# Three pairs of k-tiles by seven products in most FFN groups, with the sums of weights on GpSimd

## The chip, the core and the metric

The kernel runs on one core of one Trainium2 chip. The metric is device time in microseconds; three runs of the kernel before took 1980.76, 1980.84 and 1981.82 us, median 1980.84. The core's engines are named in the profile PE (TensorE, matmuls) with PEld (its weight loads), DVE (VectorE), ACT (ScalarE), POOL (GpSimd) and SP (SyncE, which here only issues loads and stores).

## The reference: one decoder block

On 256 positions of width 2048, all in fp32, one layer is computed:

```python
h = h + 0.5 * swiglu(rms_norm(h, ffn1_norm), ffn1_w_gu, ffn1_w_down)
h = h + hybrid_mixer(rms_norm(h, mix_norm), w_in, ..., w_out)
h = h + 0.5 * swiglu(rms_norm(h, ffn2_norm), ffn2_w_gu, ffn2_w_down)
h = h + sigmoid(rms_norm(h, ple_norm) @ ple_w_gate) * (p @ ple_w_proj)
out = rms_norm(h, final_norm)
```

`swiglu(x)` splits `x @ w_gu` into a gate and an up half of 5632 columns each and gives `(silu(gate) * up) @ w_down`. The two FFNs are most of the work, and the change concerns them alone.

## The kernel before

**Precision.** Every fp32 operand of a large matmul is split in two pieces of the type fp32r, a rounded copy "hi" and the difference "lo". A product of two operands is three matmuls: hi by hi, hi by lo, lo by hi. For weights this is `weight_pair` (L57): a load of 128x2x512 weights (a pair of k-tiles, 512 columns, 512 KB) into `raw`, a copy `whi` on ScalarE (L68) and a difference `wlo` on VectorE (L69). There are four buffers for `raw` and three each for `whi` and `wlo`.

**Groups.** An FFN is a list of groups (`plan`, L325). A gate/up group computes 512 columns of the gate and the 512 matching ones of up, for all 256 positions: 2 column blocks x 2 halves of the positions, four PSUM banks, with 8 pairs of k-tiles per block. The 11 such groups stand in three parts (`PARTS`, L27) of 3, 4 and 4; after each part two down groups multiply that part's hidden columns (12 or 16 pairs of k-tiles over two blocks) into 1024 columns of the output each. A plain pair is 2 k-tiles x 2 halves of the positions x 3 = 12 matmuls (L445 to L447).

**Seven products.** For the first `NS` = 2 pairs of k-tiles of a group the eight block products (2 halves of the positions x 2 k-tiles x 2 column blocks) are replaced by seven products of sums, in Strassen's manner: four sums of the activations, four of the weights, and additions of results into the PSUM banks. Each of the seven is 3 matmuls per pair of k-tiles (L311 to L313). The first two gate/up groups of FFN 1 and the first of FFN 2 have no such products.

- `halves` (L369) makes the activations' sums `S` on VectorE (L375, L382) and their pieces `Sh` and `Sl` (L385, L386), once for the FFN's input and once for the first hidden block of each part.
- `Group.load` (L263) loads the raw weights of the pairs into `R0` and `R1` with four 512 KB loads (L268). `all_sums` (L270) is a generator: each step yields the pieces `shi` (ScalarE, L277) and `slo` (VectorE, L278, two buffers each) of one product's weights; between the steps stand four additions on VectorE (L282), one of them into `R0`, one into `R1`, two into a tile `t2`.
- `product` (L300) issues the matmuls of one product and, after products 2, 3 and 4, the additions of one bank to another: a copy `part` on ScalarE (L318), an addition on VectorE (L319).

**The order.** A group's seven products are issued among the plain pairs of the group ahead of it, from that group's fourth pair on, one behind each pair. The list `order` names all weights of the kernel in the order of their use: pairs, sums and loads of raw weights. `next_weights` (L76) hands out the next one and prepares up to three pairs and two sums ahead. `lanes` holds generators for the work beside the matmuls; each is advanced by one step per pair. The framework puts the instructions of one engine in the order in which they are ready by its own plan, so `shi` of a coming group's first product stands on ScalarE ahead of `whi` of pairs that come earlier in `order`. Each engine then runs its instructions in that order. All loads of weights are issued from SP's queue.

Of the kernel before, what the change touches and what calls it, by code (L numbers as in the profile page):

```python
# [28 lines left out]
NS = 2  # L29
# [8 lines left out]
def block_kernel(ctx, tc, a, out):  # L38
# [37 lines left out]
    def next_weights():  # L76

        ahead = min(LEAD, done[1] // 2)
        while done[0] < len(order):
# [4 lines left out]
            if kind == "load":  # L84
                src.load()
# [153 lines left out]
    class Group:  # L239
# [8 lines left out]
        def __init__(self, kind, part, src, ns, bank, nb=0):  # L248
            self.kind, self.part, self.src, self.ns, self.nb, self.bank = kind, part, src, ns, nb, bank
            self.last = part == len(PARTS) - 1  # L250
# [12 lines left out]
        def load(self):  # L263
            fp = current[0]
            self.raw = [fp.tile([P, NS, 2, NB], F32, tag=f"R{b}", name=f"R{b}") for b in range(2)]
            for g in range(NS):
                for b in range(2):
                    nc.sync.dma_start(out=self.raw[b][:, g], in_=self.src[b][g])  # L268

        def all_sums(self):  # L270

            fp = current[0]

            def halved(w):
                hi = fp.tile([P, NS, NB], F32R, tag="shi", name="shi", bufs=2)
                lo = fp.tile([P, NS, NB], F32R, tag="slo", name="slo", bufs=2)
                nc.scalar.copy(hi, w)  # L277
                nc.vector.tensor_tensor(out=lo, in0=w, in1=hi, op=ALU.subtract)  # L278
                return hi, lo

            def add(out, x, y):
                nc.vector.tensor_tensor(out=out, in0=x, in1=y, op=ALU.add)  # L282
# [12 lines left out]
            ws = halved(b21)  # L295
            add(t2, t2, b21)
            yield ws
            yield halved(b22)
            yield halved(t2)

        def product(self, i):
# [4 lines left out]
            out = (c11, c21, c12, c22, c11, c12, c21)[i]  # L306
            whi, wlo = next_weights()
            for g in range(NS):
                xh, xl = sides[self.kind](i, g)
                st, sp = i < 4 and g == 0, i < 4 and g == NS - 1  # L310
# [18 lines left out]
    def plan(n):  # L329

        gu, down = a["w_gu" + n], a["w_down" + n]
        groups = []
        for p, (i0, i1) in enumerate(PARTS):
            for i in range(i0, i1):
                groups.append(Group("gu", p, [[gu[2 * i + b][g] for g in range(KD // 2)] for b in range(2)],
                                    NS if i > (n == "1") else 0, len(groups) % 2))
            for nb in (0, 2):
                groups.append(Group("dn", p, [[down[nb + b][g] for g in range(2 * i0, 2 * i1)] for b in range(2)],
                                    NS, len(groups) % 2, nb))
        made = []  # L340
        for i, group in enumerate(groups):
            group.follower = follower = groups[i + 1] if i + 1 < len(groups) else None
            first = 3 if i else 8
            at = []
            if follower is not None and follower.ns:
                free = len(group.plain) - 2 - first
                at = [first + min(j, j * free // 7) for j in range(7)]
            todo = []
            for j, (b, g) in enumerate(group.plain):
                if at and j == max(at[0] - 5, 0):  # L350
                    order.append(("load", follower))
                todo.append(("plain", (b, g)))
                order.append(("pair", group.src[b][g]))
                for x in range(7):
                    if at and at[x] == j:
                        todo.append(("seventh", x))
                        order.append(("sum", follower))
            made.append((group, todo))
# [10 lines left out]
    def halves(kind, hi, lo, wait=0):  # L369

        for _ in range(wait):
            yield
        fp = current[0]
        x = fp.tile([P, 2, 4, P], F32, tag="tT", name="tT").rearrange("p t q y -> p (t q y)")
        nc.vector.tensor_tensor(out=x, in0=hi.bitcast(F32).rearrange("p k x -> p (k x)"),  # L375
                                in1=lo.bitcast(F32).rearrange("p k x -> p (k x)"), op=ALU.add)
        x = x.rearrange("p (g j t y) -> p g j t y", g=NS, j=2, t=2)
        a11, a12, a21, a22 = (x[:, :, j, t, :] for t in range(2) for j in range(2))
        s = fp.tile([P, 4, NS, P], F32, tag="S", name="S")
        for o, y, z, op in ((0, a21, a22, ALU.subtract), (1, s[:, 0], a11, ALU.subtract),  # L380
                            (2, a21, a11, ALU.subtract), (3, s[:, 1], a12, ALU.add)):
            nc.vector.tensor_tensor(out=s[:, o], in0=y, in1=z, op=op)  # L382
        sh = fp.tile([P, 4, NS, P], F32R, tag="Sh" + kind, name="Sh")
        sl = fp.tile([P, 4, NS, P], F32R, tag="Sl" + kind, name="Sl")
        nc.scalar.copy(sh, s)  # L385
        nc.vector.tensor_tensor(out=sl, in0=s, in1=sh, op=ALU.subtract)  # L386

        def side(i, g):
            if i in (0, 4, 6):
                k, t = 2 * g + (i > 0), i // 6  # L390
# [822 lines left out]
```

## Time and profile before

The profiled execution took 1982.68 us, of which the profile's span is 1981.0. How many instructions of each kind there are and what they cost is asked of the trace by line, engine and shape; "mean" is the time from the start to the end of one instruction, and consecutive ones overlap somewhat. The four additions of L282 have a row each.

| what | count | mean ns | busy us |
|---|---|---|---|
| `whi`, ACT L68, 128x1024 | 583 | 1053 | 613.3 |
| `wlo`, DVE L69, 128x1024 | 583 | 1221 | 710.5 |
| `shi` of raw weights or sums in `R`, ACT L277 | 155 | 1054 | 163.3 |
| `slo` of the same, DVE L278 | 155 | 1222 | 189.3 |
| additions to `R` and `t2`, DVE L282 | 4 x 31 | 1203 to 1225 | 37.3 to 38.0 each |
| additions between banks, DVE L319 | 124 | 693 to 694 | 84.9 |

In the page's rows of 40 slices each digit is a tenth of the slice's time in which the engine was busy; PEclk is the granted clock of TensorE, which is full in every slice. POOL's row holds one 1 and 39 zeros, so GpSimd is all but idle. In rows of waits the first name is the waiting instruction's, the second the one that released it, then come the total, the number of times and the longest, in us.

### The profile page before, as it was taken

The numbers are of one execution on the slowest core, as the hardware profiler recorded it, in microseconds if no ns is written. First come the engines' busy times: TensorE is split into PE (matmuls) and PEld (weight loads), VectorE is DVE, ScalarE is ACT, GpSimd is POOL, SyncE is SP. The second block draws the span as 40 slices with busy tenths as digits, with TensorE's granted clock in tenths as the row PEclk, the third lists the DMA queues.
The fourth block names the chain that finished last, engine by engine and source line by source line (L and its number), as shares of the span: only waits on it lengthen the run. The fifth ranks groups of instructions, "written<-read, shape, count | busy, mean of one in ns | idle before, by whom it ended". The sixth has DMA issues, their size and how long they took to land. (4 is left out here: it accounts for less than half of the span.)

```text
span 1981.0 us, 24832 instructions
## 1 busy us (share of the span) xinstructions
PE 1961.9 (99%) x9022; PEld 1621.5 (82%) x9022; DVE 1507.4 (76%) x1803; ACT 1116.1 (56%) x1441; POOL 30.1 (2%) x46
## 2 busy tenths in 40 slices
PE   9999999999999999999999999999999999999998
PEld 7888888888888888878878888888888888888887
DVE  6878788777887766794786677888787877887655
ACT  6655555555555557654545455665565555655654
POOL 0000000000000000000100000000000000000000
PEclk9999999999999999999999999999999999999999
DMA  9666667756667665555564786665667656665764
GB/s 329 225 222 212 217 209 227 237 186 212 230 215 226 203 210 163 175 179 193 171 206 148 248 269 209 228 230 195 215 217 245 213 192 210 225 225 198 241 206 151
DMA packets 163228, 421.64 MB, mean 213 GB/s; under 512 B 20512, under 2 KB 59424, under 8 KB 162976
## 3 DMA queue, kind: packets, MB, share of 16 engines
q1 hardware_dynamic: 161952, 418.58, 64.2%
q10 hardware_dynamic: 1152, 1.47, 0.2%
q8 instruction: 71, 1.16, 0.2%
q14 instruction: 53, 0.43, 0.1%
HBM read 397.96 MB, written 22.02 MB: 212 GB/s over the span
## 5 line engine op out<-in xcount | busy, mean ns | idle before, releaser
L68 ACT CAST whi<-raw 128x1024 fp32r<-128x1024 f32 (+1 forms) x585 | 614.5, 1052 | 716.8 <-PE u L447 168.4
L69 DVE TENSOR_TENSOR wlo<-raw,whi 128x1024 fp32r<-128x1024 f32 (+1 forms) x585 | 711.9, 1220 | 372.0 <-ACT whi L68 370.9
L446 PE MATMUL g<-wlo,nTh 128*128 128x512 f32 x552 | 216.0, 391 | 0.4 <-DVE wlo L69 0.4
L445 PE MATMUL g<-whi,nTh 128*128 128x512 f32 x552 | 215.2, 391 | 0.7 <-ACT whi L68 0.7
L447 PE MATMUL g<-whi,nTl 128*128 128x512 f32 x552 | 215.8, 391 | 0.0
L445 PE MATMUL u<-whi,nTh 128*128 128x512 f32 x552 | 214.7, 389 | 0.0
L446 PE MATMUL u<-wlo,nTh 128*128 128x512 f32 x552 | 214.7, 389 | 0.0
L447 PE MATMUL u<-whi,nTl 128*128 128x512 f32 x552 | 214.7, 389 | 0.0
L445 PE MATMUL d<-whi,hTh 128*128 128x512 f32 x512 | 199.1, 389 | 1.0 <-ACT hTh L414 1.0
L446 PE MATMUL d<-wlo,hTh 128*128 128x512 f32 x512 | 199.2, 389 | 0.0
L447 PE MATMUL d<-whi,hTl 128*128 128x512 f32 x512 | 199.2, 389 | 0.0
L278 DVE TENSOR_TENSOR slo<-R,shi 128x1024 fp32r<-128x1024 f32 x155 | 189.3, 1222 | 12.6 <-ACT shi L277 2.7
L277 ACT CAST shi<-R 128x1024 fp32r<-128x1024 f32 x155 | 163.3, 1054 | 34.7 <-PE d L313 14.2
L103 PE MATMUL pj<-whi,nTh 128*128 128x512 f32 x448 | 179.5, 401 | 0.0
L104 PE MATMUL pj<-wlo,nTh 128*128 128x512 f32 x448 | 176.0, 393 | 2.3 <-DVE wlo L69 2.1
L105 PE MATMUL pj<-whi,nTl 128*128 128x512 f32 x448 | 175.3, 391 | 0.0
L446 PEld LDWEIGHTS g<-wlo,nTh 128*128 128x128 f32 x552 | 104.0, 188 | 23.7 <-DVE wlo L69 2.1
L445 PEld LDWEIGHTS g<-whi,nTh 128*128 128x128 f32 x552 | 104.0, 189 | 22.6 <-ACT whi L68 1.0
L447 PEld LDWEIGHTS g<-whi,nTl 128*128 128x128 f32 x552 | 104.0, 188 | 21.9 <-DVE nTl L153 0.4
L447 PEld LDWEIGHTS u<-whi,nTl 128*128 128x128 f32 x552 | 103.6, 188 | 21.6
L446 PEld LDWEIGHTS u<-wlo,nTh 128*128 128x128 f32 x552 | 103.6, 188 | 21.5
L445 PEld LDWEIGHTS u<-whi,nTh 128*128 128x128 f32 x552 | 103.6, 188 | 21.5
(301 smaller groups left out, 3028.3 us busy)
## 6 DMA issues: line engine op xcount, KB each, us to landing
raw<-in_w_gu SPq DMA_DIRECT2D x275, 512.0 KB, 4.2
raw<-in_w_down SPq DMA_DIRECT2D x128, 512.0 KB, 3.7
raw<-in_w_in SPq DMA_DIRECT2D x112, 512.0 KB, 3.6
R<-in_w_gu SPq DMA_DIRECT2D x76, 512.0 KB, 5.4
R<-in_w_down SPq DMA_DIRECT2D x48, 512.0 KB, 5.6
scr<-tb SPq DMA_DIRECT2D x74, 256.0 KB, 4.0
raw<-in_w_out SPq DMA_DIRECT2D x32, 512.0 KB, 4.2
raw<-in_w_pg SPq DMA_DIRECT2D x32, 512.0 KB, 4.4
```

Of the source, the lines that this page charges most:

```text
L68: nc.scalar.copy(hi[:, j, :], raw[:, j, :])
L69: nc.vector.tensor_tensor(out=lo[:, j, :], in0=raw[:, j, :], in1=hi[:, j, :], op=ALU.subtract)
L103: nc.tensor.matmul(outs[t], xh[:, c], whi[:, j, :], start=st, stop=False)
L104: nc.tensor.matmul(outs[t], xh[:, c], wlo[:, j, :], start=False, stop=False)
L105: nc.tensor.matmul(outs[t], xl[:, c], whi[:, j, :], start=False, stop=sp)
L277: nc.scalar.copy(hi, w)
L278: nc.vector.tensor_tensor(out=lo, in0=w, in1=hi, op=ALU.subtract)
L445: nc.tensor.matmul(out, xh[:, c], whi[:, j, :], start=st, stop=False, skip_group_check=True)
L446: nc.tensor.matmul(out, xh[:, c], wlo[:, j, :], start=False, stop=False, skip_group_check=True)
L447: nc.tensor.matmul(out, xl[:, c], whi[:, j, :], start=False, stop=sp, skip_group_check=True)
```

## The change

- `NS` becomes 3: three pairs of k-tiles go by seven products in all gate/up groups that have products, and in the down groups of the two parts of four; the down groups of the first part stay at two (`NS_DOWN`). A product is then 9 matmuls, and a group of 16 pairs has 10 plain pairs.
- The weights of those pairs are laid out in memory so that each of the four quarters (k-tile j of the pair, column block b) of all pairs is one load of 128x1536 (768 KB), tiles `R00` to `R11`. The quarters of a group are loaded while the group two places ahead of it computes, behind products 5 and 6.
- The seven products come in another order, and the weights' sums are made in place in the quarters, without `t2`; the four additions are issued on GpSimd. Both additions that used to follow products 2 and 3 in the banks now follow product 2, and the two of product 4 follow product 3.
- Products start behind the third pair of the group ahead.
- `halves` goes through its operands two pairs at a time, and its results for the FFN's input and for the hidden columns share one buffer, so they are made anew when the kind changes: at the last gate/up group and at the second down group of a part.

```diff
-NS = 2
+NS = 3
+NS_DOWN = tuple(3 if i1 - i0 == 4 else 2 for i0, i1 in PARTS)
...
+        def load(self, j, b):
+            self.raw[j, b] = raw = current[0].tile([P, NS, NB], F32, tag=f"R{j}{b}", name="R")[:, 0:self.ns]
+            nc.sync.dma_start(out=raw, in_=self.quarters[b][j])
+        def loads(self):
+            return [("load", lambda j=j, b=b: self.load(j, b)) for j, b in ((0, 1), (1, 0), (0, 0), (1, 1))]
...
-            def add(out, x, y):
-                nc.vector.tensor_tensor(out=out, in0=x, in1=y, op=ALU.add)
-            (b11, b21), (b12, b22) = ([r[:, :, j, :] for j in range(2)] for r in self.raw)
-            ws = halved(b11)
-            add(b11, b11, b12)
-            t2 = fp.tile([P, NS, NB], F32, tag="t2", name="t2")
-            add(t2, b11, b22)
-            yield ws
-            yield halved(t2)
-            ws = halved(b11)
-            add(b12, b12, b22)
-            yield ws
-            yield halved(b12)
-            ws = halved(b21)
-            add(t2, t2, b21)
-            yield ws
-            yield halved(b22)
-            yield halved(t2)
+            def add(x, y):
+                nc.gpsimd.tensor_tensor(out=self.raw[x], in0=self.raw[x], in1=self.raw[y], op=ALU.add)
+            for q, sum_ in (((0, 0), ((0, 0), (0, 1))), ((0, 0), ((0, 0), (1, 1))), ((0, 0), ((0, 1), (1, 1))),
+                            ((0, 1), ((0, 0), (1, 0))), ((1, 0), None), ((0, 0), None), ((1, 1), None)):
+                ws = halved(*q)
+                if sum_:
+                    add(*sum_)
+                yield ws
...
-            out = (c11, c21, c12, c22, c11, c12, c21)[i]
+            out = (c11, c12, c21, c22, c11, c21, c12)[i]
...
             if i == 2:
                 add(c21, c11, ALU.add)
+                add(c12, c21, ALU.subtract)
             elif i == 3:
-                add(c12, c21, ALU.subtract)
-            elif i == 4:
                 add(c21, c22, ALU.subtract)
                 add(c22, c12, ALU.add)
...
-            first = 3 if i else 8
+            after = groups[i + 2] if i + 2 < len(groups) else None
...
+                first = 2 if group.ns else 8
+                at = [first + j * (n_plain - 1 - first) // 7 for j in range(7)]
+                if not group.ns:
+                    loads.setdefault(max(at[0] - 5, 0), []).extend(follower.loads())
+                if after is not None and after.ns:
+                    for x, one in zip((5, 6, 7, 7), after.loads()):
+                        loads.setdefault(at[x] if x < 7 else min(at[6] + 1, n_plain - 1), []).append(one)
...
-        sh = fp.tile([P, 4, NS, P], F32R, tag="Sh" + kind, name="Sh")
-        sl = fp.tile([P, 4, NS, P], F32R, tag="Sl" + kind, name="Sl")
+    def halves(kind, his, los, ns, wait=0):
+        sh = fp.tile([P, 4, NS, P], F32R, tag="Sh", name="Sh")
+        sl = fp.tile([P, 4, NS, P], F32R, tag="Sl", name="Sl")
+        for g0 in range(0, ns, 2):
...
+                if dn and group.nb and not group.last:
+                    lanes.add(1, halves("gu", *nT, NS))
+                elif not dn and group.follower.kind == "dn":
+                    lanes.add(1, halves("dn", hTh[i0:], hTl[i0:], NS_DOWN[group.part]))
```

More of the change, by code (lines that the diff above doesn't have):

```diff
@@ L329, in plan, with sources @@
     def plan(n):
[L331 removed]
+        def sources(name, blk):
+            q, pairs = a[name + "q"][blk], a[name][blk]
+            return [q[:, :, g, :].rearrange("j p n -> p j n") for g in range(q.shape[2])] + \
+                [pairs[g] for g in range(pairs.shape[0])], q
         groups = []
@@ L357, in plan @@
                         order.append(("sum", follower))
+                order.extend(loads.get(j, []))
             made.append((group, todo))
@@ L479, in ffn @@
                             lanes.advance(0)
-                        if len(hTh) - 1 == PARTS[group.part][0]:
-                            lanes.add(0, halves("dn", th, tl))
         return nxt
```

89 lines of the change are left out of this document (45 added, 44 removed).

## The prediction

> **What bounds the kernel now.** I read the page's busy shares first, then a table of three stretches that are each one FFN group long, then the groups of instructions, the waits and the short timelines below.
>
> ```profile
> span 1981.0 us, 24832 instructions
> ## 1 busy us (share of the span) xinstructions
> PE 1961.9 (99%) x9022; PEld 1621.5 (82%) x9022; DVE 1507.4 (76%) x1803; ACT 1116.1 (56%) x1441; POOL 30.1 (2%) x46
> ```
>
> The profiled execution took 1982.68 us, of which 1981.0 are the span; the median of the timed runs is 1980.84, so span and median can be read as one. TensorE is busy in 99% of it and waits for nobody worth naming: what takes matmuls away shortens the kernel, as long as the other engines keep up. Whether they do is seen in the stretches:
>
> ```profile
> core 0: us, PE busy (x) PEld busy (x) DVE busy (x) ACT busy (x) POOL busy (x), PEclk, DMA share, GB/s
> 191.17:222.66 31.49, 31.49 (x140) 25.75 (x138) 27.16 (x27) 17.61 (x19) 0.00 (x0) 1.00 0.62 211
> 475.62:517.78 42.16, 42.16 (x188) 34.91 (x186) 32.33 (x31) 23.08 (x25) 0.00 (x0) 1.00 0.64 205
> 1237.52:1279.68 42.16, 42.16 (x188) 34.91 (x186) 36.63 (x39) 24.89 (x28) 0.00 (x0) 1.00 0.67 224
> ```
>
> Each row runs from one group's product 0 to the next group's: a down group of the first part (12 pairs in all), a gate/up group (16 pairs) and one in which the operand sums of `halves` are made as well. TensorE is full in all three. A group of 16 pairs holds 12 plain pairs of 12 matmuls and 7 products of 6, so 186 in 42.16 us: 0.2267 us each, a plain pair 2.72. VectorE has 9.8 us to spare out of 42.2 in the second row, 4.3 out of 31.5 in the first. GpSimd does nothing there.
>
> ```profile
> DVE wlo L69 <- ACT whi L68: 370.9, 316, 3.6
> ACT whi L68 <- PE u L447: 168.4, 135, 2.0
> ```
>
> The spare time of VectorE is waiting of this kind: it waits for ScalarE's `whi`, and that for the plain pair whose buffer (one of three) it takes. So VectorE is as far ahead as buffers allow, some two pairs, and is idle because it is ahead.
>
> ```profile
> 328.94 1.06 ACT L277 CAST shi<-R 128x1024 fp32r<-128x1024 f32 x1 [0.30 <-PE u L313]
> 331.66 1.06 ACT L68 CAST whi<-raw 128x1024 fp32r<-128x1024 f32 x1 [1.66 <-PE u L447]
> ```
>
> The same holds for a sum's pieces: `shi` starts when the product that had its buffer, two products earlier, ends (L313 is a product's last matmul). Of a product with number i, copy, difference and addition therefore have to fit between the end of product i-2 and the start of product i.
>
> **TensorE's part.** The number of groups that get a third pair follows from the loads of raw weights, four a group:
>
> ```profile
> R<-in_w_gu SPq DMA_DIRECT2D x76, 512.0 KB, 5.4
> R<-in_w_down SPq DMA_DIRECT2D x48, 512.0 KB, 5.6
> ```
>
> 76/4 = 19 gate/up groups and 48/4 = 12 down groups, of which the 8 in the two parts with four column blocks get three pairs and the 4 of the first part stay at two. In each of the 27, two plain pairs go (24 matmuls) and seven products grow from 6 matmuls to 9 (21): 3 fewer, 81 in all, 81 x 0.2267 = 18.4 us. The group's TensorE time becomes 10 x 2.72 + 7 x 2.04 = 41.5 us.
>
> **VectorE's part.** What a group of it costs:
>
> ```profile
> L69 DVE TENSOR_TENSOR wlo<-raw,whi 128x1024 fp32r<-128x1024 f32 x583 | 710.5, 1221 | 371.0 <-ACT whi L68 370.1
> L278 DVE TENSOR_TENSOR slo<-R,shi 128x1024 fp32r<-128x1024 f32 x155 | 189.3, 1222 | 12.6 <-ACT shi L277 2.7
> ...
> L282 DVE TENSOR_TENSOR t<-R,R 128x1024 f32<-128x1024 f32 x31 | 38.0, 1225 | 1.0
> L282 DVE TENSOR_TENSOR R<-R,R 128x1024 f32<-128x1024 f32 x31 | 38.0, 1224 | 3.7 <-DMA R<-in_w_gu 2.8
> L282 DVE TENSOR_TENSOR R<-R 128x1024 f32<-128x1024 f32 x31 | 37.8, 1219 | 0.0
> L282 DVE TENSOR_TENSOR t<-t,R 128x1024 f32<-128x1024 f32 x31 | 37.3, 1203 | 0.0
> L319 DVE TENSOR_TENSOR d<-d,part 128x512 f32<-128x512 f32 x48 | 32.1, 693 | 0.0
> ```
>
> Removed: the four additions, 4 x 1.22 = 4.9 us, and two `wlo`, 2.4. Added: `slo` on 1536 elements instead of 1024; from 693 ns at 512 and 1222 at 1024 the slope is 1.03 ns per element, so +0.53 each, 7 x 0.53 = 3.7. The second row's 32.3 becomes 32.3 - 4.9 - 2.4 + 3.7 = 28.7 us of 41.5. Taken alone, VectorE gets lighter. ScalarE, at 23.1, loses two copies of 1.05 and gains 7 x 0.45: 24 of 41.5, no bound. The additions into PSUM (L319) stay four a group, only two of them a product earlier.
>
> **GpSimd's part.** Four additions a group of 128x1536 (128x1024 in the four small groups). No addition of that kind is in the trace. The nearest rows are its selects, one operand in, one out:
>
> ```profile
> L1054 POOL TENSOR_SCALAR_AFFINE_SELECT st<-st x16: 401/407/1017, 966.5 to 1041.7; 128x256 f32<-128x256 f32 x16
> ```
> ```profile
> L860 POOL TENSOR_SCALAR_AFFINE_SELECT dec<-dec x4: 634/637/1557, 791.9 to 950.3; 128x512 f32<-128x512 f32 x4
> ```
>
> Medians of 407 and 637 ns give 0.90 ns per element and 0.18 us fixed. A second operand is at least one more pass: 0.18 + 2 x 1.38 = 2.9 us for 1536 as the lower bound; three passes, 4.3, as the upper. I take 3.3, near the lower one, since the select's pass already holds a read and a write and only a read is added; 2.3 for 1024. The Trainium skill (GPSIMD Engine Reference, section 3.1) has a measured addition of 2048 elements at 4497 ns, from which 1536 are an estimated 3.4 us; with it the sum below would end at 2039 instead of 2031. It concludes that elementwise work belongs on VectorE, which is a rule against this change.
>
> The maxima of the same two rows, 1017 and 1557, are the reason for my forecast:
>
> ```profile
> 949.60 2.21 POOL L860 TENSOR_SCALAR_AFFINE_SELECT dec<-dec 128x512 f32<-128x512 f32 x2 [7.29 <-DVE dec L858]
> ```
> ```profile
> 950.10 1.22 DVE L69 TENSOR_TENSOR wlo<-raw,whi 128x1024 fp32r<-128x1024 f32 x1
> ```
> ```profile
> 792.84 0.40 DVE L789 TENSOR_SCALAR rq<-ss 128x8 f32<-128x8 f32 x1 [0.33 <-ACT junk L785]
> ```
> ```profile
> L789 DVE TENSOR_SCALAR rq<-ss x2: 160/282/403, 792.8 to 876.9; 128x8 f32<-128x8 f32 x2
> ```
>
> Two selects of 0.64 us took 2.21: a `wlo` began at 950.10 while the first was ending, and the second got through only after that `wlo` was done at 951.3. In the other direction a VectorE operation that takes 160 ns took 403, because it began at 792.84 while a select was running (L860's pair of 791.9). So the two engines shut each other out. The second direction is shown for one small operation of another kind only; for a `wlo` behind a GpSimd addition no row exists. The Trainium skill (SBUF — State Buffer, "Who interferes with whom") states both directions for a VectorE operation with two SBUF inputs, held for the whole instruction; the first direction agrees with the 1557 ns here.
>
> If additions exclude `wlo`, `slo` and the like, VectorE and GpSimd are one resource. Its load is 28.7 + 4 x 3.3 = 41.9 us a group against TensorE's 41.5. Little of it can overlap: VectorE works in order, so its operations on PSUM stand behind a blocked `wlo`. I add 1.0 for gaps that never pack (none at best; 4 us is what VectorE leaves free in the fullest row above, where it is ahead): 42.9, a stall of 1.4 us a group, 27 x 1.4 = 38. With the bounds of the addition the load is 40.3 to 45.9.
>
> The same by following one group, with the steps from start to start that these rows have (`wlo` 1.1, so `slo` of 1536 elements 1.7):
>
> ```profile
> 504.60 1.22 DVE L278 TENSOR_TENSOR slo<-t,shi 128x1024 fp32r<-128x1024 f32 x1
> 505.73 1.22 DVE L69 TENSOR_TENSOR wlo<-raw,whi 128x1024 fp32r<-128x1024 f32 x1
> 506.87 1.41 DVE L406 SCALAR_TENSOR_TENSOR sil<-u,rstd,sil 128x512 f32<-128x512 f32 x2
> 508.23 1.23 DVE L69 TENSOR_TENSOR wlo<-raw,whi 128x1024 fp32r<-128x1024 f32 x1
> 509.37 1.30 DVE L163 STREAM_TRANSPOSE tb<-sil 128x512 f32<-128x512 f32 x2
> ```
>
> Time is counted from the end of the previous group's product 6. TensorE wants to run plain pairs to 10.9 us, product 0 to 12.9, a pair, product 1 to 17.7, a pair, product 2 from 20.4, a pair, product 3 from 25.2. The copy for product 0 may begin when product 5 ends, at -4.8; copy and `slo` 0 are over at -1.4. Then the shared resource does: addition 0 to 2.1, a `wlo` to 3.2, gate and transposes to 5.8, `wlo`, `slo` 1 to 8.6, `wlo` to 9.7, addition 1 to 13.0, `wlo`, addition 2 to 17.5, `wlo`, `slo` 2 to 20.3, just in time, `wlo`, addition 3 to 24.8, `slo` 3 to 26.5: 1.3 us late. GpSimd's queue holds nothing else there; behind a `shi` that waits for an addition stand ScalarE's `whi` of the coming pairs, and TensorE waits for those.
>
> **The operand sums.** `halves` was made 8 times (once per FFN and per part); it is now made 12 times, since both kinds share one buffer, 10 of them for three pairs.
>
> ```profile
> L386 DVE TENSOR_TENSOR Sl<-S,Sh 128x1024 fp32r<-128x1024 f32 x8 | 9.8, 1222 | 0.0
> L375 DVE TENSOR_TENSOR tT<-hTh,hTl 128x1024 f32<-128x1024 f32 x6 | 7.3, 1220 | 0.0
> L382 DVE TENSOR_TENSOR S<-S,tT 128x256 f32<-128x256 f32 x16 | 6.8, 422 | 0.0
> ```
>
> One was 1.22 + 4 x 0.42 + 1.22 = 4.1 us and vanished in VectorE's spare time (36.63 in the third row above, TensorE full). With the third pair come about 2.6 more (0.69 + 4 x 0.3 + 0.69). The two at an FFN's start meet no additions. The other eight large ones, 6.7 us each, fall into the early part of a group, where the resource is full: none of it lost at best, all 6.7 at worst; I take half, because the lead of two pairs is there to be spent once: 8 x 3.4 = 27 us. The four small groups: 27.2 - 4.9 + 4 x 2.3 + 1.0 = 32.5 against 31.5, 4 us together.
>
> **Loads.** The same bytes in fewer pieces: four of 768 KB instead of eight of 512. A quarter can be loaded only when the previous group's last use of it is over; for quarter (0,0) that is `slo` 5, soon after product 3. At 5.4 us for 512 KB, 768 should land in about 8, some 10 us ahead of the next product 0. I cost them at nothing; it would show as waits for `R`, and moving product 0's copy by 5 us would still be covered. The three groups without products read 18 plain pairs in rows of 2 KB instead of 4: nothing, up to 1 us at the very start, where nothing covers the first pair.
>
> **The sum.** 1980.84 - 18.4 + 38 + 27 + 4 = 2031.
>
> **The rivals.** *The additions fit in.* If an addition is 2.9 us or doesn't hold VectorE, the load is 40.3 or less, the leads cover it, and what is left is 1962.4 plus at most half of the `halves` term: 1962 to 1976. For it: VectorE alone has 12.8 us of slack a group; the lock on a `wlo` is seen in one direction only. Against: the rows of 1557 and 403. Chance 0.24. *Gain and stall cancel.* A stall of 0.68 us a group pays back exactly the 18.4: time 1977 to 1985 (0.2% is about what a measurement of this kernel can tell from no change). Chance 0.06. *GpSimd gives way.* VectorE is never delayed, but an addition gets only the time between its two-operand instructions. These take 10 x 1.22 + 7 x 1.75 = 24.5 of 41.5 us, which leaves 0.41 of the time, so an addition lasts 3.3/0.41 = 8 us. Additions 1 and 2, from 8.6 us on, end at 24.6, and copy and `slo` 3 at 27.9: product 3, due at 25.2, is 2.7 us late in each of 27 groups, and 1980.84 - 18.4 + 73 = 2035. Slower as well, but with waits for GpSimd while `wlo` stays at 1.22; it decides from 6.6 us an addition. Chance 0.13.
>
> **How the numbers follow.** The forecast, both exclude each other, has 0.57. Its own range goes from 1977 (no gaps, `halves` hidden: 0.4 x 27 + 4) to 2090 (an addition of 3.6 us, 2.6 x 27, `halves` wholly lost, 54, and 4). The range over all cases reaches down to the first rival: 1963 to 2090. Faster 0.24, same 0.06, slower 0.57 + 0.13 = 0.70.
>
> **What would show it.** TensorE with 8941 matmuls, its share under 97%, its idle time ahead of products 2 and 3 and the pairs between, waiting for `slo` and `wlo`. GpSimd with 124 additions, 108 large ones, shortest near 3.3 us, many longer by a `wlo`. The mean of `wlo` and `slo` well over 1.22 and 1.75 us. VectorE's busy share up although its work is less. Wrong if `wlo` stays at 1.22 and TensorE at 99%.

## The result, and the profile after

The changed kernel takes 2182.2 us (median; 2179.5 to 2187.8), 1.1019 times the time of before (95% interval 1.0997 to 1.1041). The direction was forecast; the loss is 201 us where 50 were forecast, and the time lies outside the range. The profiled execution took 2187.75 us.

The page's span and first part:

```profile
span 2186.0 us, 24628 instructions
...
PE 2008.4 (92%) x8941; PEld 1637.2 (75%) x8941; DVE 1697.4 (78%) x1709; ACT 1142.3 (52%) x1401; POOL 488.9 (22%) x170
```

The 81 matmuls are gone, but TensorE is busy 46 us *longer* than before and idle for 178 us instead of 19. Both have to be explained. The groups of the instructions concerned, with total, mean ns and idle time ahead:

```profile
L71 DVE TENSOR_TENSOR wlo<-raw,whi 128x1024 fp32r<-128x1024 f32 x529 | 785.5, 1492 | 236.5 <-ACT whi L70 234.1 <-DMA tT<-scr 1.4
...
L287 POOL TENSOR_TENSOR R<-R 128x1536 f32<-128x1536 f32 x108 | 417.9, 3869 | 871.7 <-DVE slo L283 798.0 <-DMA raw<-in_w_down 40.7 <-DMA R<-in_w_gu1q 22.3
...
L283 DVE TENSOR_TENSOR slo<-R,shi 128x1536 fp32r<-128x1536 f32 x189 | 394.1, 2086 | 165.6 <-ACT shi L282 165.1
...
L397 DVE TENSOR_TENSOR Sl<-S,Sh 128x1024 fp32r<-128x1024 f32 x12 | 45.5, 3790 | 0.0
```

`wlo` has gone from 1221 to 1492 ns, `Sl` from 1222 ns to 3790. There are 108 large additions, as forecast, 3.87 us on average. Where TensorE waits is said by the waits:

```profile
PE g L464 <- DVE wlo L71: 85.1, 25, 6.3
...
PE d L464 <- DVE wlo L71: 44.2, 10, 7.3
```

It waits for `wlo` of plain pairs (L464), in 35 stretches of up to 7.3 us, 129 us together. For `slo`, which the prediction had it wait for at products 2 and 3, it waits 7 us in all. One group from product 0 to product 0, then three stretches of it (columns: us, busy time of PE, PEld, DVE, ACT and POOL with the number of instructions, granted clock, DMA share, GB/s):

```profile
551.09:599.00 47.91, 43.39 (x185) 35.48 (x184) 39.66 (x25) 24.10 (x23) 14.82 (x4) 0.96 0.52 178
581.87:589.85 7.98, 7.98 (x37) 6.60 (x36) 7.51 (x2) 3.49 (x3) 6.57 (x2) 1.00 0.20 66
589.85:594.78 4.93, 0.41 (x3) 0.00 (x1) 4.93 (x5) 1.04 (x1) 3.43 (x1) 1.00 0.00 0
594.78:599.00 4.22, 4.22 (x12) 3.37 (x13) 3.40 (x4) 0.00 (x0) 0.00 (x0) 0.60 0.72 241
```

The group takes 47.9 us where 42.9 were forecast. It loses them at one place: product 6 ends at 581.87, three plain pairs run at full speed, the fourth stands still for 4.9 us, and then its remaining matmuls, 2.5 us of work, take 4.2 at a clock of 0.60. Product 0 starts 17.1 us after product 6's end instead of 10.9. What VectorE and then GpSimd did meanwhile, from the timeline (start, duration, engine, line, tiles; in brackets the idle time before and who ended it):

```profile
580.96 4.18 DVE L71 TENSOR_TENSOR wlo<-raw,whi 128x1024 fp32r<-128x1024 f32 x1 [0.54 <-ACT whi L70]
585.61 4.53 DVE L283 TENSOR_TENSOR slo<-R,shi 128x1536 fp32r<-128x1536 f32 x1 [0.47 <-ACT shi L282]
590.06 1.40 DVE L418 SCALAR_TENSOR_TENSOR sil<-u,rstd,sil 128x512 f32<-128x512 f32 x2
591.38 3.35 DVE L71 TENSOR_TENSOR wlo<-raw,whi 128x1024 fp32r<-128x1024 f32 x1
```
```profile
580.56 7.96 POOL L287 TENSOR_TENSOR R<-R 128x1536 f32<-128x1536 f32 x2 [20.30 <-DVE slo L283]
590.22 3.43 POOL L287 TENSOR_TENSOR R<-R 128x1536 f32<-128x1536 f32 x1 [1.70 <-DVE slo L283]
```

In 14 us VectorE finishes two `wlo`, one `slo` and two small operations (one row): all three large ones take 3.4 to 4.5 us instead of 1.2 or 1.7, each shut out by an addition. The first GpSimd row is *two* additions, one directly behind the other: the first of the group, and the one of quarters (0,1) and (1,1), which the prediction's walk had third (its addition 2). It can run there because only the second addition has to wait for `slo` 1 (the "lo" piece of product 1's weights), whose source it overwrites. Of ScalarE:

```profile
584.09 1.49 ACT L282 CAST shi<-R 128x1536 fp32r<-128x1536 f32 x1 [3.16 <-POOL R L287]
585.48 1.05 ACT L70 CAST whi<-raw 128x1024 fp32r<-128x1024 f32 x1
```

The copy for product 1 waits for the first addition, and `whi` of the last plain pair ahead of product 0 stands behind it. On VectorE that pair's `wlo` (591.38) stands behind `slo` 1 (585.61). This `wlo` is what TensorE waits for until 594.78.

### The profile page after: what moved, and what is told of

It is laid out like the page before. It is cut to its first block, busy times and chain, and to the rows that moved or that the text cites. A ratio compares the mean times of both kernels' runs of the same rounds, so it can differ in the third digit from the quotient of the medians.

```text
span 2186.0 us, 24628 instructions
## 1 busy us (share of the span) xinstructions
PE 2008.4 (92%) x8941; PEld 1637.2 (75%) x8941; DVE 1697.4 (78%) x1709; ACT 1142.3 (52%) x1401; POOL 488.9 (22%) x170
## 5 line engine op out<-in xcount | busy, mean ns | idle before, releaser
L71 DVE TENSOR_TENSOR wlo<-raw,whi 128x1024 fp32r<-128x1024 f32 (+1 forms) x531 | 786.9, 1489 | 237.0 <-ACT whi L70 234.6
L70 ACT CAST whi<-raw 128x1024 fp32r<-128x1024 f32 (+1 forms) x531 | 553.2, 1049 | 560.1 <-PE g L465 159.4
L287 POOL TENSOR_TENSOR R<-R 128x1536 f32<-128x1536 f32 (+1 forms) x124 | 459.8, 3708 | 996.1 <-DVE slo L283 922.1
L283 DVE TENSOR_TENSOR slo<-R,shi 128x1536 fp32r<-128x1536 f32 (+1 forms) x217 | 436.5, 2013 | 168.9 <-ACT shi L282 167.7
L282 ACT CAST shi<-R 128x1536 fp32r<-128x1536 f32 (+1 forms) x217 | 309.5, 1428 | 275.6 <-POOL R L287 121.4
L464 PE MATMUL g<-wlo,nTh 128*128 128x512 f32 x476 | 202.8, 426 | 85.1 <-DVE wlo L71 85.1
L464 PE MATMUL d<-wlo,hTh 128*128 128x512 f32 x448 | 182.1, 406 | 44.2 <-DVE wlo L71 44.2
L464 PE MATMUL u<-wlo,nTh 128*128 128x512 f32 x476 | 185.4, 390 | 0.0
L463 PE MATMUL u<-whi,nTh 128*128 128x512 f32 x476 | 185.3, 389 | 0.0
L465 PE MATMUL u<-whi,nTl 128*128 128x512 f32 x476 | 185.3, 389 | 0.0
L464 PEld LDWEIGHTS g<-wlo,nTh 128*128 128x128 f32 x476 | 96.7, 203 | 115.9 <-DVE wlo L71 95.7
L464 PEld LDWEIGHTS d<-wlo,hTh 128*128 128x128 f32 x448 | 87.7, 196 | 66.5 <-DVE wlo L71 48.2
L463 PEld LDWEIGHTS d<-whi,hTh 128*128 128x128 f32 x448 | 87.3, 195 | 24.5 <-ACT whi L70 6.1
```

Source lines behind the costliest of these rows:

```text
L70: nc.scalar.copy(hi[:, j, :], raw[:, j, :])
L71: nc.vector.tensor_tensor(out=lo[:, j, :], in0=raw[:, j, :], in1=hi[:, j, :], op=ALU.subtract)
L287: nc.gpsimd.tensor_tensor(out=self.raw[x], in0=self.raw[x], in1=self.raw[y], op=ALU.add)
L463: nc.tensor.matmul(out, xh[:, c], whi[:, j, :], start=st, stop=False, skip_group_check=True)
L464: nc.tensor.matmul(out, xh[:, c], wlo[:, j, :], start=False, stop=False, skip_group_check=True)
L465: nc.tensor.matmul(out, xl[:, c], whi[:, j, :], start=False, stop=sp, skip_group_check=True)
```

## The experiments

Two theories to begin with. *Exclusion:* an addition on GpSimd and a two-operand instruction of VectorE shut each other out. *Queue:* the chain through a third engine is slow and its waits block ScalarE's queue, whoever reads what. Later the question is why exclusion costs three times what was forecast for it.

### Which of the parts costs: E1, E2, E3

**E1** makes the additions on VectorE:

```diff
-                nc.gpsimd.tensor_tensor(out=self.raw[x], in0=self.raw[x], in1=self.raw[y], op=ALU.add)
+                nc.vector.tensor_tensor(out=self.raw[x], in0=self.raw[x], in1=self.raw[y], op=ALU.add)
```

> The four additions of weights go back to VectorE, all else as changed. Exclusion (GpSimd's additions and VectorE's two-operand instructions shut each other out): VectorE's own load is 28.7 + 4 x 1.75 = 35.7 us of 41.5 a group, so TensorE is full again and the time is 1962 to 1975; wlo back at 1.22 us. Queues (what costs is the wait of the next copy for a 3.4 us addition, with the coming pairs queued behind it): the same, since a VectorE addition takes 1.75. Rest (the third pair, the quarter loads or the operand sums made anew cost, whatever the engine): over 2050.

Measured: 1964.47 us, 0.9914 times before (0.9897 to 0.9931), the fastest of the kernels that compute the layer. Its page's first part, and the group of `wlo`:

```profile
span 1962.2 us, 24517 instructions
...
PE 1943.1 (99%) x8941; PEld 1607.1 (82%) x8941; DVE 1626.9 (83%) x1833; ACT 1152.8 (59%) x1401; POOL 29.2 (1%) x46
...
L71 DVE TENSOR_TENSOR wlo<-raw,whi 128x1024 fp32r<-128x1024 f32 x529 | 641.4, 1218 | 177.4 <-ACT whi L70 176.0
```

1980.84 - 18.4 = 1962.4 was the forecast of the matmuls alone. The third pair, the quarter loads and the operand sums made twelve times cost some 2 us by themselves, less than the spread of the four runs (1962.9 to 1965.8). The whole loss, 218 us, comes with the engine of the additions.

**E2** keeps them on VectorE and lets GpSimd read as much, for nobody:

```diff
+                spare = act.tile([P, NB], F32, tag="junk", name="spare", bufs=1)
+                for g in range(self.ns):
+                    nc.gpsimd.tensor_tensor(out=spare, in0=lo[:, g].bitcast(F32), in1=self.raw[1, 0][:, g], op=ALU.add)
```

> As the run before (additions on VectorE, right results), but behind every one of them GpSimd reads the same amount: an addition of slo and a raw quarter into a spare tile, in pieces of 512 elements, whose result nobody uses. Exclusion: VectorE's 35.7 us and GpSimd's 13.4 no longer fit into 41.5 a group, 27 x 7.6 = 205 us on top of 1962, so 2120 to 2200, wlo near 1.5 us. Queues: nobody waits for GpSimd, so 1962 to 1985.

Measured: 2238.85 us (one run), more than expected. Nothing on the way to TensorE needs GpSimd's result here, apart from the buffers that it reads, and yet the time rises by 274 us over E1. Those buffers may be a part of it, which isn't settled: `slo` waits only 6.7 us for GpSimd, but the copies `shi` wait 95 us for loads of `R` (17 in E1), one quarter of which GpSimd reads here. Its groups of instructions:

```profile
L290 POOL TENSOR_TENSOR spare<-slo,R 128x512 f32<-128x512 f32 x356 | 813.2, 2284 | 718.0 <-DVE slo L283 689.4 <-DVE S L398 8.5
...
L71 DVE TENSOR_TENSOR wlo<-raw,whi 128x1024 fp32r<-128x1024 f32 x529 | 755.7, 1435 | 155.7 <-ACT whi L70 154.8 <-DMA raw<-in_w_down 0.5
```

**E3** keeps GpSimd in the chain, for as long an operation, without reads (this leaves out the sums of weights):

```diff
-                nc.gpsimd.tensor_tensor(out=self.raw[x], in0=self.raw[x], in1=self.raw[y], op=ALU.add)
+                nc.gpsimd.memset(self.raw[x], 0.0)
+                nc.gpsimd.memset(self.raw[x], 0.0)
+                nc.gpsimd.memset(self.raw[x][:, 0], 0.0)
```

> GpSimd overwrites the quarter with zeros instead of adding, by three memsets that take as long as an addition (1.4 + 1.4 + 0.5 us); this leaves out the sums of weights. The wait of the next copy for GpSimd is the same as in the changed kernel, but GpSimd reads nothing. Exclusion by reads: wlo at 1.22, 1962 to 1985. Queues: the stalls ahead of product 0 stay, over 2100.

Measured: 1962.53 us (one run). The groups of instructions, and one row of ScalarE's timeline:

```profile
L71 DVE TENSOR_TENSOR wlo<-raw,whi 128x1024 fp32r<-128x1024 f32 x529 | 643.2, 1219 | 263.3 <-ACT whi L70 259.5 <-DMA raw<-in_w_down 1.5 <-DMA tT<-scr 1.4
...
L288 POOL MEMSET R<- 128x1536 f32 x108 | 149.5, 1385 | 6.2
```
```profile
506.23 1.48 ACT L282 CAST shi<-R 128x1536 fp32r<-128x1536 f32 x1 [3.02 <-POOL R L289]
```

ScalarE waits 3.0 us for GpSimd in the group shown, as it did in the changed kernel (3.2), and TensorE isn't late. Such waits are rarer here, 15 us in 9 times against 121 in 30, so E3 alone doesn't test the whole chain; with E2, where no copy waits for an addition on GpSimd, queue falls as a cause by itself. Two clears of 1.38 us and one of 0.53 leave `wlo` at 1219 ns: writing doesn't exclude, while the operations of E2, which read, do (`wlo` 1435 ns). The Trainium skill (SBUF — State Buffer, "Who interferes with whom") says just this, an exclusive lock for the whole instruction between a VectorE operation with two SBUF inputs and a GpSimd operation that reads SBUF; E2, E3 and the 4.18 us of a `wlo` agree.

### How the cost hangs on number and kind: E5, E6, E7

**E5** leaves one addition a group on GpSimd, the last, **E6** the other three:

```diff
-                nc.gpsimd.tensor_tensor(out=self.raw[x], in0=self.raw[x], in1=self.raw[y], op=ALU.add)
+                engine = nc.gpsimd if y == (1, 0) else nc.vector
+                engine.tensor_tensor(out=self.raw[x], in0=self.raw[x], in1=self.raw[y], op=ALU.add)
```
```diff
+                engine = nc.gpsimd if y != (1, 0) else nc.vector
```

> Only the last of the four additions (quarter (1,0) into (0,0)) stays on GpSimd, the others are VectorE's. By the load of a whole group, evenly shared, each addition on GpSimd costs (2182 - 1964)/4 = 54 us: 2019. By its place: this one runs behind product 1, where TensorE never waited in the changed kernel and VectorE was idle between buffers, so it should cost next to nothing: 1964 to 1972.

> The reverse: the first three additions on GpSimd, which run one after the other in the 17 us ahead of product 0, the last on VectorE. Evenly shared load: 1964 + 3 x 54 = 2128. Place: nearly all of the loss stays, 2150 to 2185.

Measured: E5 1983.06 us (1.0006 times before, 0.9996 to 1.0015), E6 2151.69 (one run). Over E1 that is 19 us for the last addition and 187 for the other three. The loss isn't shared evenly, but the last addition isn't free either: between the two expectations for E5.

**E7** takes the kernel before and moves only its own four additions to GpSimd:

```diff
             def add(out, x, y):
-                nc.vector.tensor_tensor(out=out, in0=x, in1=y, op=ALU.add)
+                nc.gpsimd.tensor_tensor(out=out, in0=x, in1=y, op=ALU.add)
```

> The kernel before (two pairs, eight loads, t2) with nothing changed but the engine of its four additions of 1024 elements. By the load of a whole group (32.3 - 4.9 + 4 x 2.3 = 36.7 us of 42.2) TensorE stays full: 1978 to 1985. By place: three or four of these additions stand in the 17.7 us ahead of product 0, where VectorE is already busy 15.2; 15.2 - 4.9 + 9.2 = 19.5 us don't fit, so 2 us or more in each of 31 groups: 2030 to 2080.

Measured: 2031.03 us (one run). There is no third pair here, and the evenly spread load (expected 1978 to 1985) is refuted; the time lies at the lower edge of what the place of the additions gave. One of the four additions, and `wlo`:

```profile
L69 DVE TENSOR_TENSOR wlo<-raw,whi 128x1024 fp32r<-128x1024 f32 x583 | 760.0, 1313 | 386.4 <-ACT whi L68 385.6
...
L282 POOL TENSOR_TENSOR t<-t,R 128x1024 f32<-128x1024 f32 x31 | 102.3, 3299 | 34.8 <-DVE slo L278 34.8
```

### The clock: E4, E8

The changed kernel and E1 have the same 8941 matmuls, but TensorE is busy 2008.4 us in one and 1943.1 in the other. Of the changed kernel, behind the stall shown:

```profile
589.87 0.39 PE L463 MATMUL g<-whi,nTh 128*128 128x512 f32 x1
594.78 0.79 PE L464 MATMUL g<-wlo,nTh 128*128 128x512 f32 x1 [4.52 <-DVE wlo L71]
595.37 0.63 PE L465 MATMUL g<-whi,nTl 128*128 128x512 f32 x1
595.79 0.63 PE L463 MATMUL g<-whi,nTh 128*128 128x512 f32 x1
```

After the idle stretch matmuls start 0.43 us apart instead of 0.23, for some 3.5 us. **E4** fills the stall with 20 matmuls of zeros behind the second plain pair of each of the 31 groups with products, so that TensorE doesn't fall idle; **E8** does it only in the 13 gate/up groups that a gate/up group follows:

```diff
+                    if group.ns and one == group.plain[1]:
+                        for _ in range(20):
+                            nc.tensor.matmul(group.banks[0][0:P // 2], nought,
+                                             nT[0][0][:, 0:2, :].rearrange("p k x -> p (k x)"),
+                                             start=False, stop=False, skip_group_check=True)
```
```diff
+                    if group.ns and not dn and group.follower.kind == "gu" and one == group.plain[1]:
```

> The changed kernel with 20 more matmuls of zeros (64 columns of zeros by 512, added to a bank that is in use, so the result stays) behind the second plain pair of each group with products, where TensorE idles some 5 us and its granted clock then is 0.5 for 3 to 10 us. 4.5 us of work in each of 31 groups. If the halved clock is a part of the loss: clock near 1.0 and 20 to 60 us less than the changed kernel's 2182, though work is added. If the clock costs nothing: 2182 or more.

> The changed kernel with the 20 matmuls of zeros in the 13 gate/up groups alone that are followed by a gate/up group, where the idle time stands behind the second plain pair. There the period fell from 47.9 us to about 46.6 in the run with zeros everywhere. If that was the clock: 13 x 1.3 = 17 us less than the changed kernel's 2182, 2160 to 2170. If not: 2180 or more.

Measured: E4 2191.77 us (ratio to before 1.107, 1.1034 to 1.1106), where the expectation has the clock cost nothing; E8 2164.94 (1.0925, 1.0909 to 1.0942), 17 us *less* than the changed kernel, with 13 x 20 x 0.2267 = 59 us of useless matmuls in it. So the halved clock is a real part of the loss, some 1.3 us a group where the zeros fit the stall. Why E4 doesn't gain is argued, not shown: not all groups have a stall at that place which hides the zeros, 141 us of them in all. The Trainium skill (TensorE: Matmul & The Clock Gate, Part 1) gives a window of about 3.4 us, idle or busy, after which the clock changes; the 3.5 us of slow starts after 4.9 us of idleness agree.

### Place: E9, E10

Theory by now: three additions crowd into the few plain pairs ahead of product 0; more plain pairs there would help. E9 starts the products one pair later, E10 two:

```diff
-                first = 2 if group.ns else 8
+                first = 3 if group.ns else 8
```
```diff
+                first = 4 if group.ns else 8
```

> The changed kernel, four additions on GpSimd, products starting behind the fourth plain pair instead of the third (products 0 and 1 then share a pair). The additions and what they read are the same, but the stretch between product 6 and the next product 0 is 13.6 us instead of 10.9. Place: of the 5 us of idle time and 2 of slow clock in most of 27 groups 2.7 go, 2080 to 2120. Evenly shared load: 2182 as before, and no better later.

> The same with products starting behind the fifth plain pair: 16.3 us of plain pairs for the three early additions. Place: another 2.7 us a group, 2010 to 2060, if VectorE then keeps up with the products, which stand closer together (two pairs of them share a plain pair). Evenly shared load: 2182.

Measured: 2213.84 and 2205.5 us (one run each). Both missed by over 90 us, and the theory with them; why both are slower than the changed kernel, by 32 and 23 us, is open. A group of E10:

```profile
542.49 7.94 POOL L287 TENSOR_TENSOR R<-R 128x1536 f32<-128x1536 f32 x2 [17.95 <-DVE slo L283]
552.13 4.41 POOL L287 TENSOR_TENSOR R<-R 128x1536 f32<-128x1536 f32 x1 [1.70 <-DVE slo L283]
```
```profile
542.27 1.22 DVE L71 TENSOR_TENSOR wlo<-raw,whi 128x1024 fp32r<-128x1024 f32 x1
543.41 1.30 DVE L474 SCALAR_TENSOR_TENSOR h<-d,h 128x512 f32<-128x512 f32 x2
548.40 3.65 DVE L283 TENSOR_TENSOR slo<-R,shi 128x1536 fp32r<-128x1536 f32 x1 [3.69 <-ACT shi L282]
551.97 5.64 DVE L71 TENSOR_TENSOR wlo<-raw,whi 128x1024 fp32r<-128x1024 f32 x2
```

(GpSimd first, then VectorE.) The same episode, whatever comes after it: from 543.5 to 552 not one `wlo`, while TensorE uses one every 2.72 us and has two or three in hand. A longer stretch behind the episode adds no lead to the time before it.

### Order: E11 to E16

What the episode consists of is an order: which instruction stands ahead of which in three queues. These runs put the walk's order back, one step after the other. **E11** queues the third addition behind the second on GpSimd (`issue_after` fixes the order of issue on one engine and adds no wait); **E12** keeps the framework's order and cuts each addition into three pieces:

```diff
+            made = []
             def add(x, y):
-                nc.gpsimd.tensor_tensor(...)
+                if len(made) == 2:
+                    with tc.issue_after(made[1].ins):
+                        made.append(nc.gpsimd.tensor_tensor(...))
+                else:
+                    made.append(nc.gpsimd.tensor_tensor(...))
```
```diff
+                for g in range(self.ns):
+                    nc.gpsimd.tensor_tensor(out=self.raw[x][:, g], in0=self.raw[x][:, g], in1=self.raw[y][:, g], op=ALU.add)
```

> The changed kernel with one thing different: on GpSimd the third addition of a group, (0,1) with (1,1), is queued behind the second, (0,0) with (1,1), as the prediction's walk had them; in the changed kernel it ran ahead of it, directly behind the first. If that order was the failing step, the stall falls towards the walk's 1.3 to 1.4 us a group and the time to 2030 to 2090. If the stall is set by how long VectorE is shut out by the group of early additions against the two or three pairs that lie ready, whatever their order, it stays large: 2130 to 2190, with most of TensorE's idle time still ahead of product 0.

> The changed kernel with each addition of 128x1536 issued as three of 128x512, so that VectorE can get in between after some 1.2 us and not 3.5. The same elements are read. If the loss comes from whole additions shutting VectorE out in one stretch, pieces let wlo through earlier and the time falls: 2060 to 2140. If two engines that exclude each other cost their summed time however it is cut, it stays within 2160 to 2200; each piece then waits for one VectorE instruction, the additions as a whole last longer, and the copies for the sums come later.

Measured: E11 2139.63 us (ratio 1.0796, 1.078 to 1.0812), E12 2139.75 (1.0793, 1.0775 to 1.0811). Each gives back 43 us. E11 lies in the range that was to say "whatever their order": this order is a part, not the whole. E12 is just inside its range for pieces that let `wlo` through earlier (2060 to 2140).

**E13** also holds the third addition back, by an operation on 8 elements that has to wait for a coming `wlo`; **E14** does so with pieces:

```diff
                 if len(made) == 2:
+                    pairs = [v for k, v in split if k == "pair"]
                     with tc.issue_after(made[1].ins):
+                        spare = act.tile([P, NB], F32, tag="junk", name="spare", bufs=1)
+                        wait = nc.gpsimd.tensor_tensor(out=spare[:, 0:8], in0=pairs[-1][1][:, 0, 0:8].bitcast(F32), in1=self.raw[x][:, 0, 0:8], op=ALU.add)
+                    with tc.issue_after(wait.ins):
                         made.append(nc.gpsimd.tensor_tensor(...))
```

> The kernel of the order experiment, and the third addition of a group also held back: ahead of it stands a GpSimd operation on 8 elements that reads the wlo of a plain pair two places on, so that it starts about where product 0 starts and not directly behind the second. The same additions, the same elements, the same exclusion. If the loss is made by early additions crowded into the stretch ahead of product 0, the idle time ahead of product 0 falls to 0 to 2.5 us a group and the time to 2030 to 2100. If two engines that exclude each other cost their summed time wherever the additions stand, or if additions held back make product 3 late by as much as product 0 gains, it stays at 2120 to 2160.

> The same with every addition in three pieces of 512 elements per partition. If order, place and length of the lock are separate parts of one loss, it is the fastest kernel with the additions on GpSimd: 2000 to 2080, still slower than 1981. If the pieces only replace what the order gave, it is within 15 us of the kernel beside it.

Measured: 2135.11 us (1.0775, 1.0759 to 1.0791) and 2129.73 (1.075, 1.0732 to 1.0767). E13 missed what the crowding theory expected and lies where the summed time of the two engines was to keep it (2120 to 2160); E14 came within 15 us of E13, as pieces that only replace the order would. With the third addition out of the way the stall stays. The trace of E13 shows why, on VectorE, GpSimd and ScalarE (TensorE stands still until 528.42, for `wlo` of the last pair ahead of product 0):

```profile
515.89 1.22 DVE L71 TENSOR_TENSOR wlo<-raw,whi 128x1024 fp32r<-128x1024 f32 x1
522.01 1.76 DVE L283 TENSOR_TENSOR slo<-R,shi 128x1536 fp32r<-128x1536 f32 x1 [4.90 <-ACT shi L282]
523.69 1.28 DVE L484 SCALAR_TENSOR_TENSOR h<-d,h 128x512 f32<-128x512 f32 x2
524.89 5.75 DVE L71 TENSOR_TENSOR wlo<-raw,whi 128x1024 fp32r<-128x1024 f32 x3
```
```profile
516.11 4.35 POOL L297 TENSOR_TENSOR R<-R 128x1536 f32<-128x1536 f32 x1 [20.16 <-DVE slo L283]
523.85 3.44 POOL L297 TENSOR_TENSOR R<-R 128x1536 f32<-128x1536 f32 x1 [3.38 <-DVE slo L283]
```
```profile
520.50 1.48 ACT L282 CAST shi<-R 128x1536 fp32r<-128x1536 f32 x1 [5.36 <-POOL R L297]
521.88 2.00 ACT L70 CAST whi<-raw 128x1024 fp32r<-128x1024 f32 x2
```

That `wlo` comes last in a chain that it has nothing to do with: first addition, `shi` 1, `slo` 1, and then the second addition, which `slo` 1 releases, takes the turn at 523.85 and holds it until 527.29. VectorE is idle for 4.9 us of it. **E15** therefore queues `shi` 1 and `slo` 1 behind `whi` and `wlo` of that pair (`pair_ins` keeps the instructions of each pair); **E16** behind those of the next one, the pair between products 0 and 1:

```diff
+                if len(made) == 1:
+                    with tc.issue_after(pair_ins[-2][0]):
+                        nc.scalar.copy(hi, w)
+                    with tc.issue_after(pair_ins[-2][1]):
+                        nc.vector.tensor_tensor(out=lo, in0=w, in1=hi, op=ALU.subtract)
```
```diff
+                    with tc.issue_after(pair_ins[-1][0]):
...
+                    with tc.issue_after(pair_ins[-1][1]):
```

> The kernel with the third addition held back, and one more order of the walk restored: shi and slo of a group's product 1 are queued on ScalarE and VectorE behind whi and wlo of the last plain pair ahead of product 0, not ahead of them. If TensorE's idle time ahead of product 0 comes from that wlo standing behind the chain slo 0, addition 0, shi 1, slo 1 and then behind the next addition, most of it goes: 2030 to 2090. If it is the summed time of engines that exclude each other, the wait moves behind products 0 to 2 and the time stays at 2115 to 2150.

> The same with shi and slo of product 1 one pair later, behind whi and wlo of the pair that comes between products 0 and 1. By the chain, TensorE no longer waits ahead of product 0 at all, but the sums of products 1 to 3 come later and it waits for slo there: 2030 to 2110, and better or worse than the kernel beside it according to which of the two is longer. By the summed time: 2115 to 2150, as the other.

Measured: E15 2088.41 us (1.0541, 1.0522 to 1.056), E16 2100.21 (1.0597, 1.0581 to 1.0612). Both lie below the 2115 to 2150 of a summed time that no order changes; E15 is just inside its own range. Between the changed kernel and E15 nothing differs but the order of issue and, per group, a GpSimd operation on 8 elements that waits for a `wlo`, and 94 of the 218 us over E1 are gone. Of E15 the page's first part, rows of the waits, and one group's product 3 on TensorE, GpSimd and VectorE, a fence each:

```profile
span 2086.1 us, 24627 instructions
...
PE 1984.9 (95%) x8941; PEld 1622.3 (78%) x8941; DVE 1728.7 (83%) x1709; ACT 1136.5 (54%) x1401; POOL 576.3 (28%) x201
```
```profile
PE u L326 <- DVE slo L292: 24.5, 15, 2.6
...
PE d L326 <- DVE slo L292: 13.9, 6, 4.4
...
PE u L325 <- ACT Sh L415: 13.7, 2, 6.9
...
PE d L327 <- DVE Sl L416: 11.1, 4, 2.8
```
```profile
528.43 0.39 PE L325 MATMUL u<-shi,Sh 128*128 128x512 f32 x1
530.96 0.50 PE L326 MATMUL u<-slo,Sh 128*128 128x512 f32 x1 [2.15 <-DVE slo L292]
```
```profile
519.95 4.89 POOL L304 TENSOR_TENSOR R<-R 128x1536 f32<-128x1536 f32 x1
524.79 4.50 POOL L306 TENSOR_TENSOR R<-R 128x1536 f32<-128x1536 f32 x1
```
```profile
526.39 4.52 DVE L292 TENSOR_TENSOR slo<-R,shi 128x1536 fp32r<-128x1536 f32 x1 [0.47 <-ACT shi L291]
```

The stall ahead of product 0 is all but gone: for `whi` and `wlo` of plain pairs of the FFNs TensorE waits 13 us in the whole kernel, 141 in the changed one. It now waits at product 3, for `slo` 3, which stands behind the fourth addition: the very place of the prediction's walk, 2.15 us late where it had 1.3.

## Why the prediction was right and wrong

| kernel | span | TensorE busy | idle | over E1: idle | over E1: busy |
|---|---|---|---|---|---|
| E1 | 1962.2 | 1943.1 | 19.1 | | |
| changed | 2186.0 | 2008.4 | 177.6 | 158.5 | 65.3 |
| E11 | 2139.5 | 1999.3 | 140.2 | 121.1 | 56.2 |
| E13 | 2133.5 | 1997.9 | 135.6 | 116.5 | 54.8 |
| E15 | 2086.1 | 1984.9 | 101.2 | 82.1 | 41.8 |

All from the pages' first parts, in us; "idle" is span less busy. The prediction put 38 + 27 + 4 = 69 us of stalls on 1962.4, and nothing for the clock.

- **TensorE's 18.4 us:** right; E1 comes within 2.1 us of 1962.4.
- **Length of an addition:** right. Undisturbed it takes 3.4 us (3.43 and 3.44 above), against 3.3 taken from the selects; the Trainium skill's figure (GPSIMD Engine Reference, section 3.1) gave an estimated 3.4.
- **Exclusion in both directions:** right. Without it, in E1 and E3, nothing is lost; how much it costs is a matter of order (E15). The direction without a row before has one now, a `wlo` of 4.18 us. The rivals "the additions fit in" (1962 to 1976) and "GpSimd gives way" (`wlo` stays at 1.22) fall.
- **Loads and ScalarE at nothing:** right as loads of an engine, by E1; ScalarE's queue has a part in the order below.
- **The failing step** is "I add 1.0 for gaps that never pack", and the walk that was to confirm it. A load of 41.9 us in 41.5 says something only if the shared turn is taken in the order of need. The walk assumed an order (a `wlo` between any two additions, `slo` 1 behind a `wlo`, additions one, two, three) that no row showed and that the front of the document gave reason to doubt: the framework orders instructions by when its plan has them ready. The real queues had the third addition directly behind the first, and the last pair's `wlo` behind `slo` 1. With both put back (E11, E13, E15) idle time over E1 falls from 158 to 82 us, near the 69 forecast, and the stall is at product 3. There the terms of the sum can be read one by one: TensorE waits 43 us for `slo` (24.5 and 13.9 above, and 4.8), where the sum has 38, 26 us for `Sh` and `Sl` (13.7, 11.1 and 1.6), where it has 27, and 13 us for plain pairs, where it has nothing. That the 38 come so close is in part luck: it is 25 waits of up to 4.4 us, not 1.4 us in each of 27 groups.
- **The clock** was a term left out. By the granted clock in the traces TensorE is busy for 106 us at 0.50 in the changed kernel, for 62 in E15 and never in E1; half of that, 53 and 31 us, is what it costs. The 65 and 42 us of longer busy time in the table hold 11 to 12 us more. In the group shown a stall of 4.9 us costs 6.6.
- **The operand sums:** 27 us taken, 0 to 54 as bounds; with the additions on VectorE they cost nothing (E1), in E15 TensorE waits 26 us for them. "The two at an FFN's start meet no additions" holds for FFN 1 (`Sl` 1.22 and 0.68 us) and not for FFN 2, where the third pair's `Sl` took 4.00 us, from 1290.57, beside two additions that ran from 1286.07 to 1294.02. In the changed kernel `Sl` takes 3.79 us on average. TensorE waits there too, twice by 5.5 us, at the first gate/up group of the second part of each FFN:

```profile
PE u L306 <- ACT Sh L396: 11.1, 2, 5.5
```

Open: what the order of `shi` 1 and `slo` 1 gives without E11's and E13's changes, which wasn't tried, and what the 11 to 12 us of longer busy time are that the clock doesn't explain. E7 has such time too: TensorE is busy 17 us longer than before, at a mean clock of 0.998.

## What to carry to other kernels

Two engines that exclude each other are one resource with two queues, and its cost isn't read from the sum of their loads: find out for each wait of the bounding engine what stands ahead of it in *both* queues, in the order that the scheduler really issues, and compare the longest run without a needed result with the lead of the buffers (here 8 us against two or three pairs of 2.72). When a walk through one period assumes an order, look for the row or the listing that shows it, and price the other order as a rival. To use the saving in TensorE's work, E1 is the version: additions on the engine that already had room, 1964.47 us.

## What the runs showed that was not expected

- GpSimd clears of the same total length as an addition don't disturb VectorE at all (E3: `wlo` 1219 ns), while reads whose result nobody needs cost 274 us (E2, later loads of `R` included).
- Useless matmuls made the kernel faster: 13 x 20 of zeros, 59 us of work, 17 us less time (E8).
- Cutting an addition into thirds (E12) gave as much as the better order (E11), 43 us each, but both together with the held-back third addition only 52 (E14), as if they repaired the same episode.
